# A routed mixture-of-experts block: the gather takes the bare one-hot slots, the norm's factor is applied by slot, and the first expert product is placed ahead of the rest of the gather

## The chip, the cores and the metric

The kernel runs on one core of a Trainium2 chip. The metric is device time in microseconds (us), the median over runs. Three runs of the kernel before took 422.84, 423.73 and 423.84 us. Engines are named as in the profile: PE (TensorE, with PEld for its weight loads), DVE (VectorE), ACT (ScalarE), POOL (GpSimd) and SP (SyncE, whose queue SPq issues all the large DMAs).

## The reference, cut to what matters

One layer over 256 tokens of width 1024: a norm, one wide input projection, two attention branches, an output projection, a residual sum, and then this:

```python
h2 = rmsnorm(x, norm_ffn_g)                      # x * r2 * g_ffn, r2 one number per token
group_logits = h2 @ w_router_group + b           # 8 groups
g_sel = argmax(group_logits)                     # one group per token
in_group = (h2 @ w_router_expert + b)[g_sel]     # 4 experts in it
top_vals, top_idx = top_k(in_group, 2)
combine = softmax(top_vals) * softmax(group_logits)[g_sel]   # on 2 of 32 experts
for e in range(32):
    hid = silu(h2 @ w_gate[e]) * (h2 @ w_up[e])  # 1024 -> 256
    out += (hid @ w_down[e]) * combine[:, e]     # 256 -> 1024
return rmsnorm(x + out, final_norm_g)
```

The factor r2 is one number per token. It multiplies a whole row of h2, so it can be multiplied in after the products with w_gate and w_up.

## The kernel before, in words

The weights come in slabs, most of 1 MB (128 rows by 2048 floats). `take` hands out the next slab and issues the loads that its place in SBUF allows. The 96 slabs of the experts (`w_moe`) go through a ring of 22 places. The load of a new slab waits until PE has read the slab that held the place. SPq issues in a fixed order, so one load that waits holds up all behind it. The 22 places are filled while the attention still runs, and the load of the 23rd slab waits for the first expert product.

Between attention and experts lies the routing. Tokens are two tiles of 128 rows, t = 0 and 1. `last_product` is the end of the output projection; `added` adds the residual (DVE); `turned` transposes (PE) and copies out (ACT); `logits` multiplies with the router's weights; `inv_root` makes `r2`; `chosen(t)` is a chain of nine small DVE instructions from the logits (`lg`) to the chosen experts (`sel`). A triangular product (`cum`) counts the tokens per expert, `place_of` turns this into slots, and `slots` compares the slot numbers with 1 to 32 to give the one-hot matrix `P_` (128 tokens by 4 experts of 32 slots). A second instruction in `slots` makes `Pr`, the same matrix times `r2`: DVE does it for group 0, POOL for the others. `gather(c, t, p)` multiplies half a row of x2 (c = 0 or 1, 512 of 1024 columns) with `Pr`. `kept_tokens` multiplies with the norm's gain and writes `tok`.

Then come 8 groups of 4 experts. `gate_up(n, c, w)` multiplies the 32 tokens of expert n with one slab (half c of the contraction) and takes 16 passes on PE; with c = 1 it ends in a copy `Gs` (ACT). `hidden` folds and applies silu, `places` makes the transposed slots with the weights, `down` uses four slabs of `w_down`, and `combine` adds to the output banks `OA`. `residual(i)` writes x2 into those banks, eight times. `gather` for the next group stands behind the last `gate_up` of a group. `heat` is a bf16 matmul whose result is not used.

PE, ACT and DVE follow the order of the program text in this stretch (`manual_schedule`); the slabs of group 0 are used in the order expert 0 half 0, expert 0 half 1, expert 1 half 0.

Of the kernel before, what the change touches and what calls it, by code (L numbers as in the profile page):

```python
# [78 lines left out]
def block_kernel(ctx: ExitStack, tc: tile.TileContext, a, out, cap=CAP):  # L79
# [99 lines left out]
    for i in range(NG * PER_GROUP):  # L179
        off = i * 128 * 2048  # L180
        slabs.append((a["w_moe"][off:off + 128 * 2048].rearrange("(p n) -> p n", n=2048), 2048))
# [695 lines left out]
    Pr = wk.tile([128, 2, GRP], F32, tag="P0", name="Pr", bufs=1)  # L877
# [5 lines left out]
    def slots(grp, t, eng):  # L883
# [6 lines left out]
        yield  # L890

    def placed(t, cum):
        place_of(t, cum)
        yield
        yield from slots(0, t, nc.vector)
# [4 lines left out]
    def gather(c, t, p):  # L900

        for k in range(4 * c, 4 * c + 4):
            kk = k - 4 * c
            nc.tensor.matmul(p[:, kk * GRP:(kk + 1) * GRP], x2[:, t, k * 128:(k + 1) * 128], Pr[:, t],  # L904
                             start=(t == 0 and kk == 0), stop=(t == 1 and kk == 3))

    def kept_tokens(c, p):

        nc.vector.tensor_mul(tokens[c], p.rearrange("p (k s) -> p k s", k=4), bc(g_ffn[:, 4 * c:4 * c + 4], GRP, axis=2))  # L909
# [37 lines left out]
    urgent.enter_context(tc.manual_schedule(engines={mybir.EngineType.Activation, mybir.EngineType.DVE}))  # L947
# [6 lines left out]
    logits(0, 4, 1)  # L954
# [15 lines left out]
    in_turn(inv_root(ss2[:, 1, 1:2], D, "n21", early[1], r2[:, 1:2], True), chosen(0))  # L970
# [73 lines left out]
    quarters = [slice(32 * j, 32 * j + 32) for j in range(4)]  # L1044

    def gate_up(n, c, w):
# [134 lines left out]
    with in_order, tc.manual_schedule(engines={mybir.EngineType.Activation, mybir.EngineType.DVE}):  # L1181
        for grp in range(NG):
            if grp + 1 < NG:
                for t in range(2):
                    for _ in slots(grp + 1, t, nc.gpsimd):
                        pass
            for e in range(EPG):
# [13 lines left out]
                if n == 0:  # L1201
                    weigh()
# [3 lines left out]
                if n == 1:  # L1206
                    for i in range(4, 8):
                        residual(i)
            if grp + 1 < NG:
                for c in range(2):  # L1210
                    p = pss("gx")
                    for t in range(2):
                        gather(c, t, p)
                    kept_tokens(c, p)
            hidden(EPG * grp + EPG - 1)()
            places(grp)()
# [123 lines left out]
```

## Time and profile before

| what | value |
|---|---|
| median of the runs | 423.73 us |
| profiled execution | 422.87 us |
| its span (first to last instruction) | 421.1 us |
| PE busy | 391.6 us |
| DVE, ACT, POOL busy | 205.3, 184.1, 27.0 us |
| DMA | 135.00 MB, mean 321 GB/s |

The 1.77 us between the profiled execution's time and its span lie outside the first and last instruction. The shares of busy time are means over stages with different limits. A PE shown as busy is not PE at its peak. The clock is given as a share of full speed (1.00 is 2.4 GHz, 0.50 is 1.2 GHz).

### The profile page before, as it was taken

What the parts mean: (1) busy time and instruction counts of PE and PEld (TensorE: products, weight loads), DVE (VectorE), ACT (ScalarE), POOL (GpSimd) and SP (SyncE); (2) the same over time, 40 slices, a digit from 0 to 9 for tenths busy, and PEclk for the clock granted to TensorE, in tenths of its full rate; (3) what the DMA queues carried; (4) which work ended last, traced back from release to release, by engine and by line L of the source; (5) the groups of instructions that cost most, each with busy time, mean ns of one, the idle gap of its engine ahead of it and who ended that gap; (6) DMA issues with size and microseconds to landing.
All of it is one profiled execution on the core that took longest, in us unless ns stands there. A gap on an engine that the chain in (4) does not pass through costs nothing.

```text
span 421.1 us, 8166 instructions
## 1 busy us (share of the span) xinstructions
PE 391.6 (93%) x3288; PEld 287.8 (68%) x3288; DVE 205.3 (49%) x546; ACT 184.1 (44%) x403; POOL 27.0 (6%) x30
## 2 busy tenths in 40 slices
PE   6999999999999999999999999999999788688880
PEld 3888888888867877888886857575767363364540
DVE  2889689989858665866571212121303021020033
ACT  4876588578857765575442122122122111121143
POOL 0880000000000000000000010101010001000000
PEclk9999999999999999999999999999999996998996
DMA  7995673748544489679867999999999999999962
GB/s 251 401 362 210 244 297 127 264 158 354 199 159 160 184 297 349 229 291 360 319 253 285 422 421 420 421 419 419 418 420 420 421 418 420 421 420 419 415 251 105
DMA packets 20639, 135.00 MB, mean 321 GB/s; under 512 B 2418, under 2 KB 2930, under 8 KB 5620
## 3 DMA queue, kind: packets, MB, share of 16 engines
q1 hardware_dynamic: 20596, 134.42, 80.9%
q8 instruction: 28, 0.46, 0.4%
q14 instruction: 15, 0.12, 0.1%
HBM read 133.36 MB, written 1.05 MB: 319 GB/s over the span
## 4 chain that ended last, share of the span: by engine, by line
PE 75%; DMA 20%; DVE 2%; ACT 1%; issue 0%; SPq 0%; DVEq 0%; ACTq 0%
DMA w<-in_w_moe 19%; PE a L301 13%; PE a L302 13%; PE a L303 13%; PE G L1056 9%; PE gx L904 5%; PE Y L1097 5%; PE OA L1111 3%; PE G L1072 3%; PE s L318 2%; DMA w<-in_w_att 1%; PE o L603 1%; PE t L543 1%; PE t L649 1%; PE o L661 1%; PE t L455 1%
## 5 line engine op out<-in xcount | busy, mean ns | idle before, releaser
L302 PE MATMUL a<-r 128*128 128x512 f32 (+1 forms) x244 | 93.7, 387 | 0.0
L303 PE MATMUL a<-r 128*128 128x512 f32 (+1 forms) x244 | 92.2, 383 | 0.0
L301 PE MATMUL a<-r 128*128 128x512 f32 (+1 forms) x244 | 84.0, 386 | 1.1 <-ACT r L297 1.0
L1056 PE MATMUL G<-w,tok 128*32 128x256 f32 x1024 | 68.5, 394 | 12.1 <-DMA w<-in_w_moe 12.1
L297 DVE SCALAR_TENSOR_TENSOR r<-w,ident,r 128x512 fp32r<-128x512 f32 (+2 forms) x79 | 62.5, 806 | 14.7 <-ACT r L297 14.5
L297 ACT ACTIVATE r<-w,ident 128x512 fp32r<-128x512 f32 (+2 forms) x79 | 56.8, 751 | 24.5 <-PE a L303 22.5
L1056 PEld LDWEIGHTS G<-w,tok 128*32 128x32 f32 x1024 | 29.2, 111 | 37.8 <-issue 14.0
L301 PEld LDWEIGHTS a<-r 128*128 128x128 f32 x244 | 45.0, 188 | 10.4 <-ACT r L297 1.5
L302 PEld LDWEIGHTS a<-r 128*128 128x128 f32 x244 | 45.9, 188 | 8.7 <-DVE r L297 0.5
L303 PEld LDWEIGHTS a<-r 128*128 128x128 f32 x244 | 45.8, 188 | 8.4 <-issue 0.2
L1078 DVE TENSOR_TENSOR P<-G,P 128x64 f32<-128x64 f32 x32 | 7.2, 225 | 78.7 <-ACT P L1077 78.7
L1077 ACT ACTIVATE P<-G 128x64 f32<-128x64 f32 x32 | 7.2, 224 | 70.5 <-PE G L1072 70.5
L1097 PE MATMUL Y<-w,P 128*32 128x256 f32 x512 | 31.0, 382 | 3.2 <-DMA w<-in_w_moe 3.2
L1062 ACT COPY Gs<-G 128x256 f32<-128x256 f32 x32 | 11.9, 372 | 50.1 <-PE G L1056 50.1
L297 DVE SCALAR_TENSOR_TENSOR ysb<-Y,ws,ysb 128x512 fp32r<-128x512 f32 (+1 forms) x18 | 12.5, 692 | 41.2 <-PE OA L1111 21.5
L904 PEld LDWEIGHTS gx<-Pr,x 128*128 128x128 f32 x256 | 29.2, 192 | 3.3 <-issue 2.9
L904 PE MATMUL gx<-Pr,x 128*128 128x128 f32 x256 | 30.7, 278 | 0.2 <-DVE Pr L889 0.2
L283 DVE TENSOR_TENSOR r<-w,r 128x512 fp32r<-128x512 f32 x32 | 21.9, 690 | 14.9 <-ACT r L282 13.2
L889 POOL TENSOR_SCALAR Pr<-P,r 128x128 f32<-128x128 f32 x14 | 8.3, 606 | 316.6 <-PE gx L904 190.8
L282 ACT CAST r<-w 128x512 fp32r<-128x512 f32 x32 | 19.9, 624 | 14.1 <-DVE r L283 7.4
L1097 PEld LDWEIGHTS Y<-w,P 128*32 128x32 f32 x512 | 15.0, 109 | 13.7 <-DMA w<-in_w_moe 3.4
L909 DVE TENSOR_TENSOR tok<-gx,ident 128x512 f32<-128x512 f32 x16 | 11.1, 692 | 27.1 <-PE gx L904 26.9
(223 smaller groups left out, 457.0 us busy)
## 6 DMA issues: line engine op xcount, KB each, us to landing
w<-in_w_moe SPq DMA_DIRECT2D x93, 1024.0 KB, 19.8
w<-in_w_att SPq DMA_DIRECT2D x24, 1024.0 KB, 4.9
w<-in_w_moe SPq DMA_DIRECT2D x6, 512.0 KB, 15.0
w<-in_w_att SPq DMA_DIRECT2D x3, 744.0 KB, 8.2
w<-in_w_att SPq DMA_DIRECT2D x2, 512.0 KB, 5.3
out<-r SPq DMA_DIRECT2D x2, 512.0 KB, 3.6
w<-in_w_att SPq DMA_DIRECT2D x1, 768.0 KB, 5.6
w<-in_w_att SPq DMA_DIRECT2D x2, 372.0 KB, 5.9
```

The source lines that it names most:

```text
L282: nc.scalar.copy(hi, src)
L283: nc.vector.tensor_sub(lo, src, hi.bitcast(F32))
L297: return nc.scalar.mul(hi, ps, g), nc.vector.scalar_tensor_tensor(lo, ps, g, hi.bitcast(F32), op0=ALU.mult, op1=ALU.subtract)
L301: i = nc.tensor.matmul(out_, lh, rh, start=start, stop=False)
L302: nc.tensor.matmul(out_, lh, rl, start=False, stop=False)
L303: nc.tensor.matmul(out_, ll, rh, start=False, stop=stop)
L904: nc.tensor.matmul(p[:, kk * GRP:(kk + 1) * GRP], x2[:, t, k * 128:(k + 1) * 128], Pr[:, t], start=(t == 0 and kk == 0), stop=(t == 1 and ...
L1056: nc.tensor.matmul(G[quarters[2 * z + o], :256], tokens[c][:, kk + o, CAP * e:CAP * e + CAP], w[:, (kk + o) * 512 + z * 256:(kk + o) * 512 ...
L1062: nc.scalar.copy(Gs, G[:, :256])
L1072: nc.tensor.matmul(HT[:, f * 64:(f + 1) * 64], Gs[:, f * 128:(f + 1) * 128], fold, start=True, stop=True)
L1097: nc.tensor.matmul(Y[quarters[e]], hT_[:, e, f], wv[:, f, e], start=f == 0, stop=f == 1)
L1111: nc.tensor.matmul(OA[t][h][:, c0:c0 + w], pl[:, t * 128:(t + 1) * 128], v, start=False, stop=grp == NG - 1 and q0 > 0 and v is lo, skip_g ...
```

## The change

`Pr` and its 16 multiplications (2 on DVE, 14 on POOL) go. `gather` reads `P_`. The new function `factors` collects r2 by slot with two matmuls and spreads it with four small ones, and `gate_up` multiplies the evacuation `Gs` with it in place of a copy. Group 0 is written out: `gate_up(0, 0)` stands ahead of a quarter of the gather, and expert 1's half 0 comes before expert 0's half 1, so the two slabs swap their contents. `kept_tokens` for group 0 works on two experts at a time. The 14 `heat` matmuls of the routing go. The root for t = 1 stands ahead of a copy on ACT, and the logits are cut in other pieces. The first slots of t = 0 are made inside the chain `chosen(1)`. The routing's order of ACT and DVE is now kept through the expert loop without a break.

```diff
-        off = i * 128 * 2048
+        off = {1: 2, 2: 1}.get(i, i) * 128 * 2048
...
+    def factors(grp):
+        p = pss("rq")
+        for t in range(2):
+            nc.tensor.matmul(p[:, :1], P_[:, grp % 2, t], r2[:, t:t + 1], start=(t == 0), stop=(t == 1))
+        rd = wk.tile([128, EPG], F32, tag="rd", name="rd")
+        nc.vector.tensor_scalar(rd, own, p[:, :1], None, op0=ALU.mult)
+        def spread():
+            for q in quarters:
+                nc.tensor.matmul(p[q, 4:4 + EPG], rep, rd, start=True, stop=True)
+            rqs[grp] = wk.tile([128, EPG], F32, tag="rq", name="rq")
+            nc.vector.tensor_copy(rqs[grp], p[:, 4:4 + EPG])
+        return spread
...
-        eng.tensor_scalar(Pr[:, t], P_[:, grp % 2, t], r2[:, t:t + 1], None, op0=ALU.mult)
...
-    logits(0, 4, 1)
+    logits(0, 2, 1)
...
+    root = inv_root(ss2[:, 1, 1:2], D, "n21", early[1], r2[:, 1:2], True)
+    logits(4, 4, 0)
     kept = turned(4, 4, 1, 4)
-    logits(4, 4, 0)
+    logits(2, 2, 1)
...
-    residual(0)
-    residual(1)
-    heat(lgp[0], 6)
     nc.tensor.matmul(cums[0][:, :NE], tri, sel[:, 0], start=True, stop=True)
     nc.tensor.matmul(cums[1][:, :NE], ones, sel[:, 0], start=True, stop=False)
-    residual(2)
-    residual(3)
-    heat(lgp[0], 5)
-    in_turn(chosen(1))
-    in_turn(placed(0, cums[0][:, :NE]))
+    residual(0)
+    chain = chosen(1)
+    for _ in range(3):
+        next(chain)
+    in_turn(chain, placed(0, cums[0][:, :NE]))
     gx = [pss("gx") for _ in range(2)]
+    gather(0, 0, 0, gx[0])
     nc.tensor.matmul(cums[1][:, :NE], tri, sel[:, 1], start=False, stop=True)
-    heat(lgp[0], 3)
-    gather(0, 0, gx[0])
-    gather(1, 0, gx[1])
+    gather(0, 1, 0, gx[1], 0, 2)
     in_turn(placed(1, cums[1][:, :NE]))
-    gather(0, 1, gx[0])
-    gather(1, 1, gx[1])
-    for c in range(2):
-        kept_tokens(c, gx[c])
+    gather(0, 0, 1, gx[0])
+    gather(0, 1, 0, gx[1], 2, 4)
+    for i in range(2):
+        kept_tokens(0, gx[0], 2 * i, 2)
...
-            nc.scalar.copy(Gs, G[:, :256])
+            nc.scalar.mul(Gs, G[:, :256], rqs[n // EPG][:, e:e + 1])
...
+            if grp == 0:
+                gate_up(0, 0, take()[1])
+                gather(0, 1, 1, gx[1])
+                for i in range(2):
+                    kept_tokens(1, gx[1], 2 * i, 2)
+                spread = factors(0)
+                gate_up(1, 0, take()[1])
+                spread()
+                kept = gate_up(0, 1, take()[1])
+                for i in range(1, 4):
+                    residual(i)
+                kept()
+                weigh()
+                kept = gate_up(1, 1, take()[1])
+                hidden(0)()
+                kept()
+                for t in range(2):
+                    for _ in slots(1, t):
+                        pass
+                for i in range(4, 8):
+                    residual(i)
...
+                spread = factors(grp + 1)
             hidden(EPG * grp + EPG - 1)()
+            if grp + 1 < NG:
+                spread()
```

On PE, from the first gather to the fifth slab of the experts, the kernel before has these rows (w_1935, w_1937 and so on are the slabs in the order of their places; gx is the gather, G the expert product):

```order
L310 MATMUL s<-ident_r 128x256
L904 MATMUL gx<-Pr,x 128x128 x16
L1056 MATMUL G<-w_1935,tok 32x256 x8
L1056 MATMUL G<-w_1937,tok 32x256 x8
L1056 MATMUL G<-w_1939,tok 32x256 x8
L1072 MATMUL G<-cst,Gs 128x64 x2
L1056 MATMUL G<-w_1941,tok 32x256 x8
L919 MATMUL OA<-x,ident 128x256 x4
L1056 MATMUL G<-w_1943,tok 32x256 x8
```

The changed kernel has these in the same place:

```order
L922 MATMUL gx<-P,x 128x128 x4
L1007 MATMUL cum<-sel,cst 128x32
L922 MATMUL gx<-P,x 128x128 x8
L1076 MATMUL G<-w_1935,tok 32x256 x8
L922 MATMUL gx<-P,x 128x128 x4
L888 MATMUL rq<-r_2030,P 128x1 x2
L1076 MATMUL G<-w_1937,tok 32x256 x8
L894 MATMUL rq<-rd,rep 32x4 x4
L1076 MATMUL G<-w_1939,tok 32x256 x8
L939 MATMUL OA<-x,ident 128x256 x3
L1076 MATMUL G<-w_1941,tok 32x256 x8
```

Four of the sixteen gather matmuls, six new small matmuls and three of the residual's moved behind the first expert product, and four of the gather's moved ahead of the last count. In fp32 each matmul of an order row is two passes in the trace.

On PE at the end of group 0, up to the first slab of `down` (Y), the kernel before has:

```order
L1056 MATMUL G<-w_1949,tok 32x256 x8
L904 MATMUL gx<-Pr,x 128x128 x16
L1072 MATMUL G<-cst,Gs 128x64 x2
L1021 MATMUL pl<-ident,P 128x128 x2
L1097 MATMUL Y<-w_1951,P 32x256 x8
```

And the changed kernel has:

```order
L1076 MATMUL G<-w_1949,tok 32x256 x8
L922 MATMUL gx<-P,x 128x128 x16
L888 MATMUL rq<-r_2030,P 128x1 x2
L1092 MATMUL G<-cst,Gs 128x64 x2
L894 MATMUL rq<-rd,rep 32x4 x4
L1042 MATMUL pl<-ident,P 128x128 x2
L1117 MATMUL Y<-w_1951,P 32x256 x8
```

The six matmuls of the next group's factors stand in front of the first Y.

On DVE, from the middle of `chosen(1)` to the first tokens, the kernel before has:

```order
L859 TENSOR_SCALAR other<-other,gs 128x8
L861 SCALAR_TENSOR_TENSOR el<-other,lg 128x32
L864 MAX m8s<-el 128x8
L866 COPY top<-m8s 128x2
L868 MATCH_REPLACE el_2036<-top,el 128x32
L870 TENSOR_SCALAR sel<-el_2036 128x32
L881 SCALAR_TENSOR_TENSOR place<-cum,sel 128x32
L886 TENSOR_TENSOR P<-cst,place 128x128 x2
L889 TENSOR_SCALAR Pr<-P,r_2030 128x128
L881 SCALAR_TENSOR_TENSOR place<-cum,sel 128x32
L886 TENSOR_TENSOR P<-cst,place 128x128 x2
```

The changed kernel has:

```order
L860 TENSOR_SCALAR other<-other,gs 128x8
L901 SCALAR_TENSOR_TENSOR place<-cum,sel 128x32
L862 SCALAR_TENSOR_TENSOR el<-other,lg 128x32
L906 TENSOR_TENSOR P<-cst,place 128x128
L865 MAX m8s<-el 128x8
L867 COPY top<-m8s 128x2
L869 MATCH_REPLACE el_2036<-top,el 128x32
L871 TENSOR_SCALAR sel<-el_2036 128x32
L901 SCALAR_TENSOR_TENSOR place<-cum,sel 128x32
L906 TENSOR_TENSOR P<-cst,place 128x128
L928 TENSOR_TENSOR tok<-gx,ident 128x4x64 x4
```

The slots of t = 0 moved into the chain of t = 1, two of the group-1 slots moved out behind, and `Pr` is gone. SPq has the same 199 instructions in the same order.

## Rows read from the trace of the kernel before

**Rows 1.** Page, part 2: GB/s moved in each of 40 equal slices

```profile
GB/s 251 401 362 210 244 297 127 264 158 354 199 159 160 184 297 349 229 291 360 319 253 285 422 421 420 421 419 419 418 420 420 421 418 420 421 420 419 415 251 105
```

**Rows 2.** Windows: length, busy PE, PEld, DVE, ACT, POOL, clock, DMA share, GB/s

```profile
219.00:220.00 1.00, 1.00 (x11) 1.00 (x11) 0.33 (x4) 0.83 (x6) 0.00 (x0) 1.00 0.08 33
...
222.00:223.00 1.00, 1.00 (x24) 0.51 (x20) 0.61 (x1) 0.00 (x0) 0.59 (x1) 1.00 0.00 0
...
224.00:225.00 1.00, 1.00 (x16) 0.59 (x8) 0.00 (x0) 0.19 (x1) 0.00 (x0) 1.00 0.27 90
225.00:226.00 1.00, 1.00 (x18) 0.48 (x17) 0.00 (x0) 0.72 (x1) 0.00 (x0) 1.00 1.07 442
```

**Rows 3.** Timeline of SPq: start us, us, loads issued

```profile
210.71 0.43 SPq L215 DMA_DIRECT2D w<-in_w_moe  x1
...
222.94 0.33 SPq L215 DMA_DIRECT2D w<-in_w_moe  x1
...
239.32 0.33 SPq L215 DMA_DIRECT2D w<-in_w_moe  x1
```

**Rows 4.** Waits of SPq, 200 to 260 us: total us, times, longest

```profile
SPq L215 <- PE G L1056: 24.7, 13, 11.7
```

**Rows 5.** Chain that ended last: start us, us, what

```profile
233.17 3.77 PE gx L904 x32
...
253.45 3.77 PE gx L904 x32
...
382.24 18.66 DMA w<-in_w_moe
```

**Rows 6.** Timeline of the routing: start us, us, engine, line, out<-in, count

```profile
210.78 0.59 ACT L829 COPY x2T<-t 128x512 f32<-128x512 f32 x1 [0.30 <-PE t L821]
...
211.39 0.64 PE L821 MATMUL t<-ident,x 128*128 128x128 f32 x4
...
211.86 1.92 PE L838 MATMUL s<-early,x2T 128*128 128x40 f32 x16
...
212.88 0.26 DVE L852 SCALAR_TENSOR_TENSOR lg<-s,r,b_r 128x40 f32<-128x40 f32 x1 [0.47 <-PE s L838]
...
214.86 0.18 DVE L870 TENSOR_SCALAR sel<-el 128x32 f32<-128x32 f32 x1
214.96 0.25 DVE L852 SCALAR_TENSOR_TENSOR lg<-s,r,b_r 128x40 f32<-128x40 f32 x1
...
216.92 0.18 DVE L870 TENSOR_SCALAR sel<-el 128x32 f32<-128x32 f32 x1
...
217.16 0.41 PE L984 MATMUL cum<-sel,cst 128*128 128x32 f32 x2
...
217.30 0.49 DVE L886 TENSOR_TENSOR P<-cst,place 128x128 f32<-128x128 f32 x2
...
218.04 3.84 PE L904 MATMUL gx<-Pr,x 128*128 128x128 f32 x32 [0.15 <-DVE Pr L889]
...
221.03 0.69 DVE L909 TENSOR_TENSOR tok<-gx,ident 128x512 f32<-128x512 f32 x1
...
221.81 2.80 PE L1056 MATMUL G<-w,tok 128*32 128x256 f32 x48
```

**Rows 7.** Timeline, 225 to 238 us: rows that give prices

```profile
225.28 1.28 ACT L1077 ACT_TABLE_LOAD   x1 [1.09 <-PE G L1072]
226.13 1.99 PE L919 MATMUL OA<-x,ident 128*128 128x256 f32 x8
...
237.66 0.51 PE L1023 MATMUL pl<-wts,P 128*128 128x4 f32 x4
```

**Rows 8.** Windows of 2 us: the clock's fall

```profile
332.00:334.00 2.00, 1.07 (x16) 0.42 (x16) 0.15 (x1) 0.37 (x1) 0.00 (x0) 1.00 1.00 418
...
346.00:348.00 2.00, 0.68 (x16) 0.37 (x16) 0.75 (x1) 0.03 (x1) 0.00 (x0) 1.00 1.01 422
...
350.00:352.00 2.00, 2.00 (x17) 0.73 (x18) 0.00 (x0) 0.00 (x0) 0.00 (x0) 0.50 1.01 414
```

More of the change, by code (lines that the diff above doesn't have):

```diff
@@ L876, in block_kernel, with slots @@
     hT_ = shaped(P_and_hT[:, 4 * GRP:], [128, EPG, 2, CAP])
-    Pr = wk.tile([128, 2, GRP], F32, tag="P0", name="Pr", bufs=1)
+    rep = cp.tile([128, CAP], F32, name="rep")
+    nc.gpsimd.tensor_add(rep, fold[:, :CAP], fold[:, CAP:])
+    rqs = {}
+    quarters = [slice(32 * j, 32 * j + 32) for j in range(4)]
+    def factors(grp):
[10 more added lines that the diff above has]
+        return spread
     def place_of(t, cum):
         nc.vector.scalar_tensor_tensor(place[:, t], cum, 1.0, sel[:, t], op0=ALU.add, op1=ALU.mult)
-    def slots(grp, t, eng):
+    def slots(grp, t):
         dst = P_[:, grp % 2, t].rearrange("p (e s) -> p e s", e=EPG)
@@ L888, in slots @@
         yield
-        eng.tensor_scalar(Pr[:, t], P_[:, grp % 2, t], r2[:, t:t + 1], None, op0=ALU.mult)
-        yield
     def placed(t, cum):
@@ L894, in placed, with gather, kept_tokens @@
         yield
-        yield from slots(0, t, nc.vector)
+        yield from slots(0, t)
     tokens = [wk.tile([128, 4, GRP], F32, tag=f"gt{z}", name="tok", bufs=1) for z in range(2)]
-    def gather(c, t, p):
-        for k in range(4 * c, 4 * c + 4):
+    def gather(grp, c, t, p, k0=0, k1=4):
+        for k in range(4 * c + k0, 4 * c + k1):
             kk = k - 4 * c
-            nc.tensor.matmul(p[:, kk * GRP:(kk + 1) * GRP], x2[:, t, k * 128:(k + 1) * 128], Pr[:, t],
+            nc.tensor.matmul(p[:, kk * GRP:(kk + 1) * GRP], x2[:, t, k * 128:(k + 1) * 128], P_[:, grp % 2, t],
                              start=(t == 0 and kk == 0), stop=(t == 1 and kk == 3))
-    def kept_tokens(c, p):
-        nc.vector.tensor_mul(tokens[c], p.rearrange("p (k s) -> p k s", k=4), bc(g_ffn[:, 4 * c:4 * c + 4], GRP, axis=2))
+    def kept_tokens(c, p, e0=0, n=EPG):
+        es = slice(CAP * e0, CAP * (e0 + n))
+        nc.vector.tensor_mul(tokens[c][:, :, es], p.rearrange("p (k s) -> p k s", k=4)[:, :, es],
+                             bc(g_ffn[:, 4 * c:4 * c + 4], CAP * n, axis=2))
     OA = [[None, None], [None, None]]
@@ L946, in block_kernel @@
     urgent.enter_context(tc.high_priority(300))
-    urgent.enter_context(tc.manual_schedule(engines={mybir.EngineType.Activation, mybir.EngineType.DVE}))
+    by_trace = ctx.enter_context(ExitStack())
+    by_trace.enter_context(tc.manual_schedule(engines={mybir.EngineType.Activation, mybir.EngineType.DVE}))
     added(512, 512, 0, acc[1])
@@ L1043, in block_kernel @@
     pls, Gss = {}, {}
-    quarters = [slice(32 * j, 32 * j + 32) for j in range(4)]
     def gate_up(n, c, w):
@@ L1179, in final_part @@
         nc.vector.tensor_mul(ob[:, t, c0:c0 + n], OA[t][h][:, cs], g_fin[0][:, c0:c0 + n])
-    with in_order, tc.manual_schedule(engines={mybir.EngineType.Activation, mybir.EngineType.DVE}):
+    with in_order, by_trace:
         for grp in range(NG):
-            if grp + 1 < NG:
+            if 0 < grp < NG - 1:
                 for t in range(2):
-                    for _ in slots(grp + 1, t, nc.gpsimd):
+                    for _ in slots(grp + 1, t):
                         pass
-            for e in range(EPG):
+            if grp == 0:
[19 more added lines that the diff above has]
+                    residual(i)
+            for e in range(0 if grp else 2, EPG):
                 n = EPG * grp + e
@@ L1200, in block_kernel @@
                     heat(idle_bank, HEAT)
-                if n == 0:
-                    weigh()
                 kept()
@@ L1205, in block_kernel @@
                     todo.pop(0)()
-                if n == 1:
-                    for i in range(4, 8):
-                        residual(i)
             if grp + 1 < NG:
@@ L1212, in block_kernel @@
                     for t in range(2):
-                        gather(c, t, p)
+                        gather(grp + 1, c, t, p)
                     kept_tokens(c, p)
+                spread = factors(grp + 1)
             hidden(EPG * grp + EPG - 1)()
+            if grp + 1 < NG:
+                spread()
             places(grp)()
```

4 lines of the change are left out of this document (3 added, 1 removed).

## The prediction, made before the change was run

> **What bounds the kernel now.** I read the transfer rates first. In the page's slices (10.53 us each) the rate wanders between 127 and 401 GB/s for the first 22 slices and then stands at 415 to 422 until slice 38, two before the last [rows 1]. The flat part is the experts' weights. At 421 GB/s a slab of 1 MB takes 2.49 us. The chain of waits agrees: near its end it is one long piece on the loads of `w_moe` [rows 5]. Yet the same chain runs through PE earlier, so I asked how fast PE empties slabs: its gather comes once a group, at 233.17 and at 253.45 us, that is 20.28 us for 12 slabs, and DMA needs 12 x 2.49 = 29.9 us for them [rows 5]. PE has 9.6 us to spare in each group. From the moment the flow starts, the end follows from the bytes still to come.
>
> The second view is the windows around the start of that flow. Transfers die out at 219 to 220 us (33 GB/s, DMA share 0.08), are at zero at 222 to 223, and are back in full at 225.0 [rows 2]. The queue's timeline says why: SP issues a load at 210.71 us and the next only at 222.94, and the longest wait there, 11.7 us, is on the expert product G [rows 3, 4]. All 22 places are full and the 23rd load needs the first slab read. That product starts at 221.81 us [rows 6]. From issue to full flow pass 225.0 - 222.94 = 2.06 us [rows 2, 3]. So the time is: start of the first expert product, plus a constant, so long as DMA doesn't run dry again.
>
> **The change part by part.** I work out when the first product G starts, and then whether PE still frees places in time.
>
> *Logits and roots.* Before, the first full logits are waited for by `lg` at 212.88 us, and the transposes of t = 1, which end at 212.03, stand ahead of their second half [rows 6]. Now the second half needs only the ACT copy that ends at 211.37. The 8 passes took 212.88 - 212.03 = 0.85 us, handover included, so `lg` starts near 212.3: 0.55 us earlier. The logits of t = 1 follow after transposes (0.64), copy (0.59) and 8 passes (0.85), near 214.4. The second `lg` stood at 214.96, right behind `sel` at 214.86, and moves to about 214.45 [rows 6]. The root put ahead of the copy changes nothing: the copy waits for its transposes anyway.
>
> *The chain for t = 1.* From `lg` at 214.96 to the end of `sel` at 217.10 it takes 2.14 us [rows 6]. Now two instructions stand inside it, `place` (about 0.18, as `sel`) and one slot matrix (0.49 / 2 = 0.25). They cost between nothing, if they fall into the gaps of dependent instructions, and 0.43. I take 0.2, as the chain has such gaps after every step. `sel` then ends at 216.8, 0.3 us earlier.
>
> *From `sel` to the first product.* Before: count, place, two slot matrices (one of them already for group 1) and `Pr`, gather from 218.04 for 32 passes at 0.12 us, `tok` at 221.03 for 0.69, product at 221.81 [rows 6]. The stretch from 217.10 takes 4.71 us. Now: count 0.47 (217.10 to 217.57), place and one slot matrix with handovers 0.65, 8 passes 0.96, handover 0.11, half of `tok` about 0.43 (between half of 0.69 and all of it), handover 0.09. That is 2.7, with the rounding of the handovers 2.8 us, and G starts at 219.6 instead of 221.81: **2.2 us earlier**. The 8 passes of t = 0 are hidden in the wait for `sel`. If both insertions cost in full and half a `tok` costs 0.69, it is 220.1; if they cost nothing and it takes 0.35, 219.3.
>
> *What was taken off that path stands behind it.* The residual's six passes (1.99 / 8 = 0.25 each, 1.5 us), the gather's last 8 passes (0.96) and the factors all have to run before the ninth load [rows 6, 7]. A factor costs 4 passes with a single column; the nearest row is `pl<-wts`, 4 passes in 0.51 us [rows 7]. Its spread has 8 passes with 32 columns of weights: 0.058 each by G (2.80 / 48) or 0.128 by that row, so 0.45 to 1.0; I take 0.45, as G loads weights of the same width [rows 6, 7]. Group 0 carries two factors: 2 x (0.51 + 0.45) = 1.9. Together PE has 4.4 us more to do between the first product and the first Y. No queue but PE's stands behind these matmuls, and PE is waited for by SP only.
>
> *The ninth load.* It was issued at 239.32 us, when the first Y was through [rows 3]. Now: 239.32 - 2.2 + 4.4 = 241.5, with flow from 241.5 + 2.06 = 243.6. Eight slabs from 225.0 - 2.2 = 222.8 last until 242.7. So DMA would run dry for 0.9 us where before it had 244.9 - 241.4 = 3.5 us to spare. This is what is late next. If all engines of the DMA stood still for it, the gain would be 244.9 - 243.6 = 1.3 us; if none, 2.2. The 16 engines don't run in step: at 219 to 220 us a share of 0.08, about one engine of 16, is still moving data, and the last slices fall from 415 to 251 and 105 GB/s [rows 1, 2]. The last engine sets the end, and it is the one that has work left while the others are dry. I take the middle, **1.8 us**. After this point PE has 20.28 + 0.96 = 21.2 us of work per group against 29.9 of DMA, so nothing runs dry again.
>
> *What costs nothing.* `Pr` on POOL and the slots of later groups on DVE, the factors of later groups, and `Gs` as a multiplication lie in the 9.6 us a group that PE waits for data. If that cover went, the factors would cost 7 x 0.96 us. The table loads on ACT (1.28 each) now come after the first `Gs`, two of them before expert 0's silu; I find silu done near 229, about when PE comes to the third expert's bank; a miss would delay the ninth load by as much [rows 7].
>
> The sum is made against the profiled execution: 422.87 - 1.8 = 421.1. That execution lies 0.86 below the median of the three runs, so I give 423.73 - 1.8 = **421.9 us**.
>
> **The rivals.**
>
> *The clock falls (slower).* The 14 unused matmuls that filled PE's waits in the routing are gone. The trace shows what such waits can do: after a stretch in which PE was busy 0.68 of 2 us the clock stood at 0.50 at 350 to 352 us, where it had held at 1.00 through a window with 1.07 of 2 us busy [rows 8]. Against it: gather, residual and counts still fill most of 214 to 218 us by my working, and the waits left are near 0.3 us each. Its place is the stretch from 214 us to the fourth expert product; the price is half of the time spent at 1.2 GHz. With one such spell of 6 us (my assumption) PE loses 3 us and some more by waits: the ninth load is issued at 244.6, flows from 246.7 instead of 244.9, and the kernel is 1.7 us slower, 425.4. It decides for slower once PE loses more than 1.3 us. The Trainium skill says in "TensorE: Matmul & The Clock Gate", section "A second HAM failure mode: psum-queue depth-cycling", that a PE which idles briefly but often between groups of matmuls swings between the two clocks. By that rule this rival would hold; the trace shows 1.00 in every window from 219 to 226 us, but with the filling matmuls before it, so no run here shows the bare stretch.
>
> *The gain is eaten at the ninth load (no change).* If PE's extra work is 5.5 us instead of 4.4 (spread at 1.0 each, 1.1 more), or silu is late by 1 us, the load flows from 244.6 or later, and 0.3 us or less is left for engines that run dry: 423.4. For it: the margin of 3.5 us is all used up in my own sum. Against it: the engines out of step.
>
> *The full shift (faster still).* The ninth load's wait is hidden and the inserted instructions cost nothing: 2.2 to 2.6 us, 421.3.
>
> *The change does not do what it says.* If the copy or `tok` in halves leaves the first product near 221, then 0.8 us at most: 423.0. The order on PE speaks against it, since 8 passes and not 24 stand ahead.
>
> **How the numbers follow.** My forecast 0.50, the full shift 0.12, eaten at the ninth load 0.20, does not do what it says 0.08, the clock 0.10. About 0.3%, 1.27 us, is what a measurement of this kernel can tell from no change. My forecast reaches from 1.2 to 2.3 us, so nearly all of it is faster; with the full shift that gives 0.60. The two middle cases and the part of the clock's case in which PE loses little are no change: 0.31. The rest, 0.09, is slower. The range runs from 420.5 (2.6 us of gain against the median, and the runs' spread of half a us) to 424.3, into the clock's case.
>
> **What would show it.** Right: the first G near 219.6 us and a load issued some 1.1 us behind it; full flow at 222.8; the ninth load after 241 us with a dip in the GB/s near 243; the clock at 1.00 from 210 to 230. Wrong: a clock of 0.50 there, a first G later than 220.5, or a gap of two us or more in the flow after 235 us.

## The result and the profile after

The changed kernel takes 425.96 us (median of 4 runs, 425.83 to 426.16), the kernel before 423.42 beside it: a ratio of 1.0057 [1.0038, 1.0075]. It is slower by 2.5 us, where 1.8 us of gain were predicted. Below, a ratio is always to runs of the kernel before on the same chip, with its 95% interval.

I read the changed kernel's windows around the start of the flow first (length, busy PE, PEld, DVE, ACT, POOL, clock, DMA share, GB/s).

```profile
213.00:215.00 2.00, 1.62 (x14) 1.42 (x13) 1.83 (x15) 0.59 (x1) 0.00 (x0) 0.97 1.03 410
215.00:217.00 2.00, 2.00 (x8) 1.77 (x9) 1.79 (x13) 0.00 (x0) 0.00 (x0) 0.50 0.97 410
217.00:219.00 2.00, 2.00 (x11) 2.00 (x11) 0.20 (x2) 0.00 (x0) 0.00 (x0) 0.50 0.23 94
219.00:221.00 2.00, 2.00 (x10) 2.00 (x11) 0.46 (x2) 0.00 (x0) 0.00 (x0) 0.50 0.03 12
221.00:223.00 2.00, 2.00 (x24) 1.40 (x22) 0.76 (x2) 0.00 (x0) 0.00 (x0) 0.83 0.00 0
...
225.00:227.00 2.00, 2.00 (x42) 1.15 (x31) 0.58 (x5) 0.33 (x1) 0.00 (x0) 1.00 0.92 385
...
245.00:246.00 1.00, 1.00 (x24) 0.67 (x20) 0.62 (x1) 0.34 (x1) 0.00 (x0) 1.00 0.80 262
246.00:247.00 1.00, 1.00 (x24) 0.45 (x15) 0.13 (x1) 0.56 (x1) 0.00 (x0) 1.00 0.96 393
```

Two things stand here that [rows 2] do not have. TensorE's clock is at 0.50, its lower level of 1.2 GHz, from 214.86 to 221.69 us, right where the gain was to be made; and at 245 to 246 us the flow dips to 262 GB/s. The timeline of the routing and the first product, to be held against [rows 6], shows what the clock took (start us, us, engine, line, out<-in, count).

```profile
212.66 0.26 DVE L853 SCALAR_TENSOR_TENSOR lg<-s,r,b_r 128x40 f32<-128x40 f32 x1 [0.34 <-PE s L839]
...
214.64 0.18 DVE L871 TENSOR_SCALAR sel<-el 128x32 f32<-128x32 f32 x1
...
216.76 1.92 PE L922 MATMUL gx<-P,x 128*128 128x128 f32 x8
216.99 0.18 DVE L871 TENSOR_SCALAR sel<-el 128x32 f32<-128x32 f32 x1
...
218.75 3.43 PE L922 MATMUL gx<-P,x 128*128 128x128 f32 x16
...
221.70 0.76 DVE L928 TENSOR_TENSOR tok<-gx,ident 128x256 f32<-128x256 f32 x2 [2.20 <-PE gx L922]
...
222.18 1.07 PE L1076 MATMUL G<-w,tok 128*32 128x256 f32 x16
...
231.59 0.37 PEld L1076 LDWEIGHTS G<-w,tok 128*32 128x32 f32 x12 [0.53 <-DVE P L1098]
```

Sixteen passes of the gather take 3.43 us, 0.21 each, against 0.12 in [rows 6]. Only 16 rather than 32 stand between `sel` and the first product, but it starts at 222.18 instead of 221.81.

The executions reach the routing up to 1.5 us apart, so I also count from the last matmul of the output projection. Its row, of the kernel before, the changed one, and t_after_32 (the changed kernel with its buffers elsewhere, below):

```profile
209.90 0.40 PE L303 MATMUL a<-r 128*128 128x512 f32 x1
```

```profile
210.03 0.39 PE L304 MATMUL a<-r 128*128 128x512 f32 x1
```

```profile
209.39 0.39 PE L304 MATMUL a<-r 128*128 128x512 f32 x1
```

From there to the first product pass 11.91, 12.14 and, where the clock held, 9.97 us. All eight versions of the changed kernel whose clock held in the routing have 9.97, the six whose clock fell 11.02 to 12.14, the kernel before and its variants 11.90 to 11.92. So the change brings the first product 1.94 us forward, and the fall of the clock took 2.17 us here.

The last row of the timeline is the price of ACT's table loads: PE comes to the third expert and waits 0.53 us for `P`, which DVE makes from ACT's activation, and that stands behind two of them. SP's queue says what followed (start us, us, loads).

```profile
223.31 0.33 SPq L216 DMA_DIRECT2D w<-in_w_moe  x1
...
243.78 0.33 SPq L216 DMA_DIRECT2D w<-in_w_moe  x1
```

From first to ninth load it was 239.32 - 222.94 = 16.38 us [rows 3], now 20.47. Eight slabs last 8 x 2.49 = 19.9 us, so the flow ran dry. In the kernel before, the windows in which the changed kernel dips have no dip:

```profile
245.00:246.00 1.00, 1.00 (x8) 0.55 (x11) 0.00 (x0) 0.26 (x1) 0.79 (x2) 1.00 1.09 442
246.00:247.00 1.00, 1.00 (x17) 0.42 (x15) 0.00 (x0) 0.00 (x0) 0.00 (x0) 1.00 1.02 426
```

A third difference is small and stands everywhere. Here is one long window of the steady flow, of the kernel before and then of the changed one:

```profile
256.00:400.00 144.00, 129.43 (x1550) 82.66 (x1550) 25.16 (x71) 25.33 (x68) 5.94 (x10) 0.96 1.01 420
```

```profile
256.00:400.00 144.00, 135.57 (x1648) 88.78 (x1644) 27.21 (x83) 27.44 (x67) 0.00 (x0) 0.96 1.01 418
```

The flow of the changed kernel is 0.4% slower, also in its slices:

```profile
GB/s 271 399 349 201 238 297 131 266 167 332 200 178 161 167 299 373 215 303 357 316 214 320 410 388 422 418 419 417 419 419 418 418 419 415 419 418 418 418 237 104
```

[rows 1] have 418 to 422 in most of them. The last five experiments are about it.

### The profile page after: what moved, and what is told of

Its sections match the earlier page's. It is cut to its first block, busy times and chain, and to the rows that moved or that the text cites. A ratio compares the mean times of both kernels' runs of the same rounds, so it can differ in the third digit from the quotient of the medians.

```text
span 423.6 us, 8320 instructions
## 1 busy us (share of the span) xinstructions
PE 400.9 (95%) x3370; PEld 296.1 (70%) x3370; DVE 207.5 (49%) x562; ACT 187.5 (44%) x403; POOL 18.8 (4%) x17
## 4 chain that ended last, share of the span: by engine, by line
PE 77%; DMA 15%; DVE 3%; ACT 1%; issue 1%; SPq 0%; DVEq 0%; ACTq 0%
DMA w<-in_w_moe 14%; PE a L303 12%; PE a L304 12%; PE a L302 12%; PE G L1076 11%; PE gx L922 6%; PE Y L1117 5%; PE OA L1131 3%; PE G L1092 3%; PE s L319 2%; DMA x<-in_x 1%; PE o L604 1%; PE t L544 1%; DVE tok L928 1%; PE pl L1042 1%; PE t L650 1%
## 5 line engine op out<-in xcount | busy, mean ns | idle before, releaser
L1082 ACT ACTIVATE Gs<-G,rq 128x256 f32<-128x256 f32 x32 | 15.2, 474 | 54.5 <-PE G L1076 54.5
L922 PEld LDWEIGHTS gx<-P,x 128*128 128x128 f32 x256 | 31.7, 204 | 3.5 <-issue 3.3
L922 PE MATMUL gx<-P,x 128*128 128x128 f32 x256 | 33.4, 291 | 0.0
L928 DVE TENSOR_TENSOR tok<-gx,ident 128x512 f32<-128x512 f32 (+1 forms) x18 | 11.2, 631 | 29.5 <-PE gx L922 29.5
L1092 PEld LDWEIGHTS G<-cst,Gs 128*128 128x128 f32 x128 | 17.1, 195 | 9.7 <-ACT Gs L1082 4.9
```

The costliest lines, as they stand in the source:

```text
L928: nc.vector.tensor_mul(tokens[c][:, :, es], p.rearrange("p (k s) -> p k s", k=4)[:, :, es], bc(g_ffn[:, 4 * c:4 * c + 4], CAP * n, axis=2))
L1082: nc.scalar.mul(Gs, G[:, :256], rqs[n // EPG][:, e:e + 1])
L1092: nc.tensor.matmul(HT[:, f * 64:(f + 1) * 64], Gs[:, f * 128:(f + 1) * 128], fold, start=True, stop=True)
```

## The experiments

A table first; its numbers come from the results, SP's timeline and the landings of the loads. "Distance" is from the first to the ninth load. The trace has 16 landings for each load. I read them as one for each of the 16 DMA engines, and the last as the slowest engine's; the trace does not name the engines. "dry, first" and "dry, last" say how much longer than in the kernel before (4.96 and 4.97 us) it took from the eighth load's first (last) part to the tenth load's; 0 stands for less than 0.15. The first tells how long the flow stood still, the last what the slowest engine lost. The last four columns are those of one profiled execution; in m_logits, r_after_384 and t_after_32 it took 425.09, 423.91 and 420.42 us, 1.7 to 2.0 us below the median, so these columns do not explain the median there.

```
                us      ratio [95%]              first G  distance  dry, first  dry, last
after           425.96  1.0057 [1.0038, 1.0075]  222.18   20.47     0.49        1.72
a_before_bare   423.31  1.0001 [0.9987, 1.0015]  221.97   16.38     0           0
b_heat          424.43  1.0022 [1.0005, 1.0040]  220.19   20.48     0.85        2.47
h_two           425.65  1.0047 [1.0026, 1.0067]  221.14   20.48     1.09        1.96
i_gather        426.51  1.0069 [1.0050, 1.0087]  220.84   20.48     1.11        2.23
m_logits        427.07  1.0081 [1.0057, 1.0105]  220.78   20.48     0.42        0.08
c_heat_late     425.34  1.0041 [1.0025, 1.0057]  219.78   23.06     2.33        2.45
d_late          426.84  1.0080 [1.0059, 1.0101]  222.52   21.86     1.44        1.57
e_fill38        425.27  1.0042 [1.0027, 1.0057]  222.38   20.75     1.03        2.23
f_fill19        423.79  1.0012 [0.9994, 1.0030]  222.06   18.68     0           0
g_full          422.71  0.9994 [0.9978, 1.0010]  219.41   20.42     0.46        0.43
g2_full         422.27  0.9986 [0.9969, 1.0003]  219.47   18.85     0           0
k_best          422.70  0.9984 [0.9968, 1.0000]  220.42   18.85     0           0.31
n_nofill        424.47  1.0021 [0.9999, 1.0042]  221.19   20.46     0.34        0.55
p_before_128    424.52  1.0023 [1.0012, 1.0033]  221.94   16.38     0           0
q_before_160    421.43  0.9956 [0.9939, 0.9973]  222.24   16.38     0           0
r_after_384     425.57  1.0055 [1.0037, 1.0074]  221.26   20.47     0.44        0.53
t_after_32      422.44  0.9980 [0.9960, 1.0000]  219.37   20.47     0.27        2.12
s_aligned       419.22  0.9895 [0.9875, 0.9914]  220.55   18.85     0           0
```

**Were the unused matmuls what held the clock?** Once they are taken out of the kernel before, and once put back into the changed one, at the waits for both `lg` (4 and 4), for `P` (3) and for the second count (2).

```diff
 a_before_bare, in the kernel before:
-    heat(lgp[0], 6)
-    heat(lgp[0], 5)
-    heat(lgp[0], 3)
 b_heat, in the changed kernel:
+    heat(acc[0], 4)      # ahead of each logits(4, 4, t)
+    heat(lgp[0], 3)      # ahead of the gather
+    heat(cums[0], 2)     # ahead of gather(0, 0, 1, ...)
```

> The kernel before, without the 14 filling matmuls of the routing and with nothing else changed. Theory clock (the changed kernel lost its time because TensorE's clock fell to 0.50 from 215 to 221 us, where the fillers are gone): the clock shows 0.50 somewhere between 211 and 224 us, the first expert product starts 1 to 2.5 us after 221.8 us, and the kernel takes 424.4 to 425.9 us against 423.4. Theory order (the clock does little; the time was lost because PE's work was put between the first product and the ninth load): no change beyond 0.3%, as the ninth load of the kernel before has 3.5 us to spare.

> The changed kernel with 13 filling matmuls in PE's waits of the routing (4 and 4 ahead of the last two pieces of the logits, 3 ahead of the gather's first piece, 2 ahead of its second). Theory clock: granted clock 1.00 from 205 to 245 us, first expert product at 219.6 to 220.2 us, ninth load issued at 241.2 to 241.9 us, 421.6 to 422.6 us in all. Theory order: the ninth load stays at 243 us or later and the kernel at 425 us or more.

Without them the kernel before keeps its clock in the routing and its time. These are its windows in the routing:

```profile
214.00:216.00 2.00, 1.58 (x9) 1.15 (x9) 1.72 (x12) 0.30 (x1) 0.00 (x0) 1.00 0.92 311
216.00:218.00 2.00, 1.26 (x6) 0.69 (x5) 1.72 (x11) 0.00 (x0) 0.00 (x0) 1.00 0.83 344
```

PE idles more here than in the changed kernel's 213 to 215 us (1.62 busy), and the clock stands. So their absence alone does not drop the clock. In the changed kernel with them it holds (first G 220.19), yet the kernel stays slower: 424.43 us is what neither of the two theories expected. Its queue and its dip, with the clock at 1.00 all through:

```profile
221.32 2.76 SPq L216 DMA_DIRECT2D w<-in_w_moe  x2
...
241.80 3.96 SPq L216 DMA_DIRECT2D w<-in_w_moe  x4
```

```profile
243.00:244.00 1.00, 1.00 (x25) 0.66 (x20) 0.61 (x1) 0.35 (x1) 0.00 (x0) 1.00 0.87 229
244.00:245.00 1.00, 1.00 (x24) 0.46 (x16) 0.14 (x1) 0.55 (x1) 0.00 (x0) 1.00 0.95 369
```

The ninth load at 241.80 and a dip after it are what the prediction worked out (241.5). What it cost is not: the slowest engine lost 2.47 us, about three times the 0.85 us of standing still, and kept the lag. From the tenth load's last part to the last load's pass 157.6 us, as in p_before_128 below, which has the same places and does not run dry.

**Where does the clock's fall come from?** Two unused matmuls at each logits wait; five at the gather's waits only; and no unused matmuls, but the logits in the order of before.

```diff
 h_two:     +    heat(acc[0], 2)   # ahead of each logits(4, 4, t)
 i_gather:  +    heat(lgp[0], 3)   # and heat(cums[0], 2), as in b_heat
 m_logits:  -    logits(0, 2, 1) ... logits(4, 4, 0) ... logits(2, 2, 1)
            +    logits(0, 4, 1) ... logits(4, 4, 0)   # behind the transposes
```

> The changed kernel with 4 fillers only, 2 in each of the two waits that the new pieces of the logits leave on PE (211.2 to 211.5 and 213.5 to 213.8 us). Theory waits (the new waits between the logits' pieces, not the fillers' absence behind them, let the clock fall at 214.9 us): clock 1.00, first product near 219.7 us, and 424.1 to 424.7 us as with 13 fillers. Rival (PE needs the fillers of the gather's waits as well): clock 0.50 from about 215 us, first load near 223.3 us, 425.5 to 426.2 us.

> The changed kernel with 5 fillers only in the waits of the gather (3 and 2), none at the logits. Theory waits: the clock falls at 215 us as in the changed kernel, first load near 223.3 us, 425.5 to 426.2 us. Rival: it holds, 424.1 to 424.7 us.

> The changed kernel with the logits' pieces in the order of the kernel before, without any filler. Theory waits: with no waits between the pieces the clock stays at 1.00, the first product starts at 219.8 to 220.4 us, and the ninth load's dip is left, 424.1 to 424.9 us. Rival (the fillers' absence): clock 0.50 near 215 us and 425.5 us or more.

The theory of the waits misses in all three. The clock fell in the first (216.48 to 219.89) and third (215.16 to 218.58) and held in the second. So the rival, that PE needs the unused matmuls of the gather's waits, is right about the clock each time, and about the time in h_two and m_logits. But i_gather, which held the clock in its profile, takes 426.51: a held clock is not enough. Its windows, and where its unused matmuls run:

```profile
215.00:217.00 2.00, 1.93 (x16) 1.60 (x15) 1.76 (x12) 0.00 (x0) 0.00 (x0) 1.00 0.99 365
217.00:219.00 2.00, 1.95 (x17) 1.74 (x16) 1.28 (x8) 0.00 (x0) 0.00 (x0) 1.00 0.76 311
```

```profile
210.87 0.39 PE L304 MATMUL a<-r 128*128 128x512 f32 x1
...
216.71 0.49 PE L311 MATMUL s<-ident_r 128*128 128x256 bf16 x3
```

Over all profiles, those of the versions below included, the pattern is the same: the seven changed kernels with unused matmuls at the gather's waits held 1.00 through the routing, and six of the seven without fell. It is no proof that these matmuls hold it. They start 5.84 us behind the last matmul of the output projection in i_gather, and in the changed kernel the clock fell 4.83 us behind it. And three kernels with the same instructions differ: after fell for 6.83 us, r_after_384 for 3.41, t_after_32 not at all. The windows of r_after_384 and then of t_after_32:

```profile
215.00:217.00 2.00, 1.93 (x8) 1.41 (x8) 1.76 (x12) 0.00 (x0) 0.00 (x0) 0.62 1.01 422
217.00:219.00 2.00, 2.00 (x11) 2.00 (x11) 0.36 (x3) 0.00 (x0) 0.00 (x0) 0.53 0.41 164
```

```profile
215.00:217.00 2.00, 1.62 (x13) 1.22 (x12) 1.43 (x9) 0.00 (x0) 0.00 (x0) 1.00 0.94 369
217.00:219.00 2.00, 1.92 (x16) 1.73 (x16) 0.60 (x3) 0.00 (x0) 0.00 (x0) 1.00 0.31 131
```

What lets the clock fall stays open.

**Less work between first and ninth load.** The residual's products 1 to 7 are put behind the first group's last down product, with the unused matmuls of b_heat and without.

```diff
-                for i in range(1, 4):        # and range(4, 8) further down
-                    residual(i)
+            if grp == 0:                     # behind the last down product
+                for i in range(1, 8):
+                    residual(i)
```

> As the run with fillers, and the seven residual products that stood between the first expert product and the ninth load now stand behind the four down slabs of group 0. Both theories in one: with the clock at 1.00 the first product is at 219.6 to 220.2 us, the ninth load goes out near 238 us, nothing runs dry, and it takes 421.0 to 421.6 us. If the residual products' place is worth nothing once the clock holds, it equals the run with fillers alone within 0.2 us.

> The changed kernel without fillers, with the seven residual products behind the down slabs of group 0. The clock falls as in the changed kernel and the first load goes out near 223.3 us. Theory clock: only the ninth load's part comes back, the ninth load near 240.3 us, 423.9 to 424.4 us. Theory order: all of it comes back, 422.5 us or less.

Both miss. The residual's products had been the cover of ACT's chain from `Gs` through two table loads to the activation; bare, PE stands still behind it for 3.35 us, and in that wait the clock falls (228.09 to 234.92). The third expert's product in c_heat_late:

```profile
229.01 1.93 PE L1080 MATMUL G<-w,tok 128*32 128x256 f32 x16 [3.35 <-DVE P L1102]
```

So the exponentials behind these table loads were taken early, right behind `placed(1)`: g_full is c_heat_late with that, g2_full has 8 unused matmuls instead of 13, and k_best is g2_full with `residual(1)` to `(3)` back in PE's wait.

```diff
+    weigh_exp()          # neg and the four Exp of weigh(), behind placed(1)
-    heat(acc[0], 4)      # g2_full: 2, 2, 2, 2
+    heat(acc[0], 2)
```

> The changed kernel with the 13 fillers, the exponentials of the routing's weights (and their table load) put ahead of the gather on ACT as far as their inputs allow, and the seven residual products behind the down slabs of group 0. Theory (clock, then the ninth load, with ACT's table loads as what kept PE waiting in the two runs that moved the residual products alone): clock 1.00 from 205 to 245 us, first product near 220.2 us, no PE wait over 1.2 us for silu, ninth load before 239 us, no dip, 421.9 to 422.5 us. Rival: the early shift of the flow is lost again elsewhere, 423.3 us or more.

> The same with 8 fillers (2 at each of the four places). If two at each place hold the clock: first product near 219.8 us and 421.5 to 422.2 us. If the clock falls to 0.50 near 215 us: first load at 222.8 us or later and 423.0 us or more.

> The version with 8 fillers and early exponentials, with three of the seven residual products put back into PE's 1.9 us wait for silu and four left behind the down slabs. Theory: clock 1.00, first product near 219.5 us, ninth load near 239.5 us, no dip, 421.6 to 422.4 us, as without the three; it beats the kernel before by 0.2 to 0.5%. If the three products cost time, the ninth load is later by up to 1.5 us and it stays in its margin.

These are the first versions of the change that are not slower than the kernel before. All three missed their expected times by 0.1 to 0.3 us: in g_full the clock fell later (228.06 to 231.47) and the distance stayed at 20.42 us. In g2_full a first product 1.9 us earlier, by the count above, and nothing dry gave 0.6 us. Something still took more than a microsecond.

**The delay of the ninth load by itself.** The kernel before with unused matmuls ahead of the first group's first down slab.

```diff
+            if grp == 0 and q == 0:
+                heat(bank, 38)       # f_fill19: 19
```

> The kernel before with 38 filling matmuls (some 4.6 us) on PE ahead of the first down slab of group 0, so that its ninth load goes out near 243.9 us instead of 239.3 and DMA runs dry for about 1.1 us. Theory restart (when the flow has to start anew, the slowest of the 16 DMA engines loses more than the idle time): full flow is back later by 2 us or more for the last landings, 425.2 to 426.5 us. Theory of the prediction (the last engine has work left and hides the idle time): at most 1.1 us are lost, 424.2 us or less.

> The same with 19 filling matmuls, some 2.3 us: the ninth load goes out near 241.6 us, which is inside its 3.5 us to spare. Both theories: no dip in the flow near 245 us and no change beyond 0.3% (423.3 to 424.2 us). If it is slower than that, the ninth load is not what decides, or the margin is smaller than worked out.

With 38 the distance is 20.75 us and the kernel 1.8 us slower (1.1 to 2.4 by the interval), as the restart theory expected; with 19 it is 18.68 and nothing can be told. Extra work on PE cost nothing that shows while the eight slabs lasted. Past them, 1.03 us without data cost at least that. The restart in e_fill38:

```profile
245.00:246.00 1.00, 1.00 (x28) 0.57 (x23) 0.14 (x1) 0.69 (x1) 0.00 (x0) 1.00 0.82 131
246.00:247.00 1.00, 1.00 (x24) 0.62 (x20) 0.61 (x1) 0.08 (x1) 0.00 (x0) 1.00 0.74 287
```

**The clock without a dry queue.** g2_full without any unused matmuls.

```diff
-    heat(acc[0], 2)      # and the other three
```

> The changed kernel with the exponentials of the routing weights taken early and all seven residual products put behind the first group's last down product, and with none of the unused matmuls. PE's work between the first and the ninth load is as in the run with eight unused matmuls, so the ninth load should come about 18.9 us behind the first, under the 19.9 us that eight slabs last. If the dry DMA queue is what costs, the time is within 0.3% of the kernel before whatever the clock does near 215 us: 422.3 if the clock holds, 423.4 to 424.3 if it falls and moves the first product to 221.5 or later (a distance over 19.9 us, because a second fall lies behind the first product, would bring the cost back). If the clock's fall is what costs, by itself and not through the dry queue, the time is 425 us or more with the clock at 0.50 near 215 us.

The clock fell twice (216.40 to 219.81 and 230.05 to 233.46), and the second fall brought the distance back to 20.46 us, so the causes did not come apart. The time, 1.0021 [0.9999, 1.0042], is below the 425 us of the clock's theory, and its runs lie from 423.16 to 427.68.

**The slower flow.** The landings gave the lead: from the first landing of the twelfth load, near 255 us, to that of the last, near 405 us, every kernel above with the change takes 151.06 to 151.29 us, the kernel before and its variants a, e and f 150.41 to 150.47. (The expectations call this 56 slabs, a count of landings that the trace shows; some are missing, and only the same stretch is compared.) The change adds a tile `rep` of 32 numbers, 128 bytes a partition. It stands ahead of the places of the slabs, which so begin at byte 14304 of a partition instead of 14176, by the addresses in the built programs. Four kernels move these places, and the work buffers behind them, by widening `b_r` with numbers that nothing uses:

```diff
-    b_r = cp.tile([128, 40], F32, name="b_r")
+    b_r = cp.tile([128, 40 + 32], F32, name="b_r")[:, :40]
 p_before_128: before, + 32 (14304)      q_before_160: before, + 40 (14336)
 r_after_384:  after, + 96 (14688)       s_aligned:    g2_full, + 8 (14336)
```

> The kernel before with 128 unused bytes a partition in front of the slabs' places, so that they start at byte 14304 of a partition, as in the changed kernel, instead of 14176; no instruction differs. Theory place: the slower flow of every kernel that has the change's tiles (151.1 us for 56 slabs from the tenth to the sixty-sixth load, against 150.4 in the kernel before and its variants) comes from where the slabs lie. Then 151.1 us here, the time 0.6 to 0.7 us above before, the last load 0.7 us later. Theory work: it comes from what PE, DVE and ACT do more in every group. Then 150.4 us and the time of before.

> The kernel before with 160 unused bytes a partition in front of the slabs' places, which then start at byte 14336, a multiple of 256 and 512. Theory place, an estimate by the rule on transactions of 256 B in the Trainium skill, page DMA: Bandwidth & Descriptors, section How a descriptor splits into AXI transactions: the 8192 B of a row are 256 beats from here, 259 from 14176 and 263 from 14304; if 4 beats are the 0.65 us between 151.1 and 150.4 us, 3 fewer beats give 149.9 us for the 56 slabs. Theory work: 150.4 us. In time 0.5 to 0.8 us below before by the first, no change by the second.

> The changed kernel with 384 unused bytes a partition in front of the slabs' places, which then start at byte 14688, as far from a multiple of 512 as those of the kernel before. Theory place: 150.4 us for the 56 slabs instead of 151.1, the time 0.7 us below the changed kernel's, so about 1.004 of before. Theory work: 151.1 us and 1.0057 of before.

> The run with eight unused matmuls, early exponentials and late residual products, with 32 more unused bytes a partition, so that the slabs' places start at byte 14336. Theory place: 149.9 to 150.4 us for the 56 slabs instead of 151.2, so 0.8 to 1.3 us less than the 422.3 it took: 421.0 to 421.5, about 0.996 of before. Theory work: 151.2 us and 422.3.

The steady flow of p_before_128, q_before_160, r_after_384 and s_aligned, in this order; the last number is GB/s.

```profile
256.00:400.00 144.00, 130.10 (x1545) 83.00 (x1544) 25.05 (x70) 24.77 (x66) 5.91 (x10) 0.95 1.01 418
```

```profile
256.00:400.00 144.00, 129.38 (x1566) 83.16 (x1565) 25.75 (x73) 26.77 (x70) 5.94 (x10) 0.98 1.01 425
```

```profile
256.00:400.00 144.00, 134.35 (x1651) 88.35 (x1651) 27.20 (x83) 27.94 (x68) 0.00 (x0) 0.98 1.01 420
```

```profile
256.00:400.00 144.00, 136.28 (x1702) 90.07 (x1694) 27.67 (x87) 30.43 (x74) 0.00 (x0) 1.00 1.01 425
```

The rate goes with the place and not with the work: 418 at byte 14304 in both kernels, 420 at 14176 and 14688, 425 at 14336. The stretch takes 151.08, 148.52, 150.58 and 148.56 us. The place alone makes the kernel before 1.0023 [1.0012, 1.0033] slower: 1.0 us, with an interval of 0.5 to 1.4 that includes the 0.67 us of that stretch. An aligned place makes it 0.9956 [0.9939, 0.9973]: more than the 0.5 to 0.8 us expected. s_aligned is the fastest kernel of all, 0.9895 [0.9875, 0.9914]. r_after_384 missed in time: its flow is as fast as before, its median is not, and its runs go from 423.82 to 427.69.

The Trainium skill, in "DMA: Bandwidth & Descriptors", section "How a descriptor splits into AXI transactions", says that a transfer is cut at multiples of 256 B and that a start off such a multiple costs beats. It words the rule for reads; here it is the place written to that moves. For a row of 8192 B that would be an estimated 256, 259 and 263 beats from bytes 14336, 14176 and 14304; the stretch measured 148.52, 150.41 and 151.08 us, in the same order. The size fits at one place alone: 1.3% and 1.7% were measured where the beats give 1.2% and 2.7%.

Last, the changed kernel itself at the aligned place (`40 + 8`):

> The changed kernel with 32 unused bytes a partition in front of the slabs' places, which then start at byte 14336, as in the aligned variant of the kernel before (0.9956 of before). Nothing else differs, so the place of the slabs is taken out of the comparison and what is left is the change's own work. If the place is 0.0023 of the loss of 0.0057 and the rest (the ninth load's delay and the clock) adds to it, this kernel is 0.0034 above the aligned kernel before, 0.9990 of before, with the 56 slabs in 148.5 us and the ninth load 20.5 us behind the first. If the place was all of it, 0.9956. An aligned place also shortens what eight slabs last, from 19.9 to about 19.6 us, so the dry stretch may be somewhat longer.

In its profile the clock held, and this is the first product that the prediction had worked out at 219.6:

```profile
219.37 1.07 PE L1076 MATMUL G<-w,tok 128*32 128x256 f32 x16
```

It takes 0.9980 [0.9960, 1.0000] against 0.9956 for the kernel before at the same place: a difference of 0.0024, 1.0 us, with intervals that overlap. The value between "place is all" (0.9956) and "place and the rest add" (0.9990) is nearer to the second, but the runs rule out neither; in its profile the slowest engine again lost 2.12 us at the ninth load.

## Why the prediction was wrong

*What bounds the kernel: right.* With the same place and nothing dry, s_aligned starts its first product 222.24 - 220.55 = 1.7 us earlier than q_before_160, and its last expert load ends 1.6 us earlier (404.94 against 406.50). The ratios, 0.9895 against 0.9956, differ by 2.6 us. The gain sought exists and is passed on to the end.

*First product 2.2 us earlier, at 219.6: near where the clock holds, 1.94 us; the clock at 1.00 in the sum: this step failed.* (219.37 in t_after_32 has luck in it, as its routing began 0.5 us early.) In the changed kernel it was 222.18: the rival "the clock falls", given 0.10, came true at its place, 214.86 to 221.69, and near its time, 425.4. The fall took 2.17 us, more than the gain. The rule cited there, from the Trainium skill's "TensorE: Matmul & The Clock Gate" and its "A second HAM failure mode: psum-queue depth-cycling", agrees with this fall, but not with a_before_bare, whose PE was busy 1.58 and 1.26 of 2 us at 1.00, nor with t_after_32, which held with the same instructions. Nor is the fall all of the price: it moves first and ninth load alike, by 2.0 us (223.31 - 221.32 and 243.78 - 241.80 against b_heat), and b_heat, with the clock held, is faster than the changed kernel by only 1.5 us and still slower than before.

*PE does 4.4 us more between first and ninth load: near, with luck* (20.47 - 16.38 = 4.1). Of the 4.1 us 0.53 is the wait for `P`, which the sum put at nothing. The two factors took about 1.0 us of PE, from start to next start, instead of 1.9. *The ninth load at 241.5, DMA dry for 0.9 us: right where the clock held* (241.80 and 0.85 in b_heat; 243.78 and 0.49 in the changed kernel).

*"The last engine sets the end, and it is the one that has work left while the others are dry. I take the middle": this step failed.* From the engines' being out of step I had concluded that a dry stretch of 0.9 us would cost half of that. The slowest engine lost 2.47 us in b_heat, 2.23 in e_fill38, 1.72 in the changed kernel: more than all of the dry time. I had the restart's price before me, 2.06 us from issue to full flow, and used it only for the start. It is no fixed price: g_full, n_nofill and r_after_384 lost 0.43 to 0.55 us in their profiles at the same distance, about what they stood still. Only m_logits lost less (0.08 of 0.42); there the engines were already 3.0 us apart at the eighth load, as my step had supposed, and 1.4 to 2.4 in the others.

The part beyond the dry time, 0.9 to 1.9 us in six profiles, is not shown to come from the restart. The last landing also falls back where nothing is dry, by 1.04 us in the kernel before at the 32nd load behind the first product, near 307 us. At the ninth and tenth load only kernels that ran dry have such a step, which speaks for the restart. Whether it is why the runs of such kernels spread over 4 to 5 us (n_nofill, r_after_384, t_after_32) wasn't tried; f_fill19, dry nowhere in its profile, spreads over 3.9.

*A term the sum lacks: the tile `rep`.* Its 128 bytes moved every slab and cost 0.67 us of the steady flow, and 1.0 us of the whole kernel in p_before_128.

*Table loads: near.* With the clock held the activation is done at 229.3 us (b_heat), where 229 was worked out. PE was there earlier, and waits 0.53 us.

In the profiled execution the sum was 421.1 us and the time 425.84, 4.7 us more. The first load came 2.56 us later than worked out: 0.36 us behind the kernel before instead of 2.2 ahead. The slowest engine lost 1.72 us, 1.3 more than the 0.4 in the sum. The slower flow is 0.67. Together that is 4.5.

So the loss of 0.0057 is the place with 0.0023, shown by itself from the kernel before, and some 0.0034 of dry queue and clock beyond what the earlier first product gives back. At the aligned place 0.0024 of this is seen, with intervals that overlap. r_after_384, back on the place's old rate, did not get the 0.0023 back in its median. Queue and clock were not parted further in the changed kernel; that a dry queue alone costs time is shown in the kernel before, by e_fill38.

## What to carry to other kernels

When a transfer queue is the bound, compare how long the loads already issued last with when the next one is issued. Work that fits in between cost nothing here; past it the slowest engine's loss counted, not the mean dry time. A small tile that is allocated ahead of large buffers moves them; where they begin is worth a test of its own before the change's work is judged (32 bytes between g2_full and s_aligned are 0.9986 against 0.9895, more than the whole change). Work moved out of the way may have been the cover of another engine's wait.

## What the runs showed of the hardware

- The place of the slabs in a partition sets the rate of their loads: 418, 420 and 425 GB/s with the first at byte 14304, 14176 and 14336.
- A queue that was dry for 0.3 to 1.1 us cost the slowest of 16 DMA engines between 0.1 and 2.5 us, and b_heat kept its lag over the remaining 157.6 us, the same stretch as in p_before_128.
- The same instructions ran through the routing with the clock at 0.50 for 6.83 us (the changed kernel), for 3.41 us (r_after_384) and not at all (t_after_32), with only places in SBUF different.
